# Retention's output and the last feed-forward with 512-wide matmuls throughout, and a feed-forward factor from two fp32r matmuls

## The chip, the cores and the metric

The kernel runs on one core of a Trainium2 chip. Its engines work side by side and are tied together by semaphores: PE (TensorE) multiplies matrices and writes to PSUM, ACT (ScalarE), DVE (VectorE) and POOL (GpSimd) work on elements, and SP issues transfers. PSUM has eight banks here of 128 x 512 float32 values. The metric is the device time of one launch in microseconds, as the median of several runs. Before the change it was 1341.47 us (three runs, 1341.17 to 1342.63).

## The reference

The program is a trunk of four layers on 256 tokens with 1024 features. Each layer does `x += mixer(RMSNorm(x))` and then `x += MLP(RMSNorm(x))`; the mixers are retention (layers 0 and 3), a convolution module (layer 1) and stick-breaking attention (layer 2). The two parts that the change touches are the output projection of retention and the feed-forward:

```python
def retention_mixer(xn, w_in, q_gain, k_gain, gn_w, gn_b, w_out):
    ...
    return (jax.nn.silu(g) * y) @ w_out          # (256, 2048) @ (2048, 1024)

def squared_relu_mlp(xn, w1, w2):                # w1 (1024, 4096), w2 (4096, 1024)
    h = jax.nn.relu(xn @ w1)
    return (h * h) @ w2

def rms_norm(x, w):
    xf = x.astype(jnp.float32)
    y = xf * lax.rsqrt(jnp.mean(xf * xf, axis=-1, keepdims=True) + EPS)
    return (y * w.astype(jnp.float32)).astype(x.dtype)
```

## The kernel before

**Split products.** Every float32 operand of a large product is held as two fp32r parts, a rounded "high" part and the rest, "low". A product is then high x high + high x low + low x high. Weights come in units of 128 x 1024 values (a chunk of two units is one transfer of 1 MB); ACT casts the high part `wh` (L357) and DVE subtracts to get the low part `wl` (L364). Activations are kept transposed, features on the partitions and the 256 tokens along the free axis, as a tile `[high 256 | low 256]`: `z0` to `z7` for the normed input (L446 on ACT, L447 on DVE), `h` for the feed-forward's middle, `y` for the mixer's result (`split`, L382 and L383).

**Two forms of one unit.** A unit of kind "b" has four blocks of 128 input features (`kk`) and two halves of 128 output features (`m`), so eight groups. `mm_b`, the narrow form, does a group as three matmuls with 256 columns each (L511, L512, L513) that all add into one half of one bank. `mm_w`, the wide form, does it as two: `wl` times the high half, 256 columns (L527), and `wh` times both halves at once, 512 columns (L531). The wide form keeps the two halves of the result apart, so a pair of output blocks needs two banks, and `sum_w` adds them afterwards: per bank one ACT copy (L574) and one DVE addition (L575) into an SBUF tile. Both forms stream 768 columns a group.

**Banks.** Two pools of four banks each: `acc` for the large products and `mis` for everything else (transposes, column sums, scores).

**Retention's output** (the end of `retention`, L881 to L889) has four pairs of output blocks, `p` = 0 to 3, and four units each. The units come in the order of `OUT_ORDER`: p 0 and 1 in turn over the four `kb`, then p 2 and 3 in turn. Pairs 0, 1 and 2 are wide in two `acc` banks each, pair 3 is narrow in one. Since `acc` has four banks, pair 2 takes the banks of pair 0. `evac` (in `out_begin`) adds the result to `x` (L899) and makes the next norm's `z` tiles and squares (`norm_pair`); pair 3 makes `z6` and `z7`, which the feed-forward needs for the last quarter of its input features.

**The feed-forward** (`ffn`) makes 16 pairs of 256 middle features from two units each, and then in layers 0 to 2 four pairs of 8 units with `w2` (pairs 0 to 2 wide, pair 3 narrow in layer 0 and three quarters wide, by `pair_x`, in layers 1 and 2). The norm's factor is not applied to the input. In layers 0 to 2 it is multiplied onto the result of `w2`; `norm_rb` makes it, called while pair 2 is traced: POOL adds the two halves of the squares (L485), a float32 matmul with a matrix of -1 sums over the partitions and spreads the sum (L487), and DVE makes the reciprocal. In the last layer it is applied in `act` (L617) to each pair of the middle; it is made by `norm_r` (column sums, L407, after pair 0) and `bcast` (four small matmuls, L414, inside pair 2). Pairs 0 and 1 are computed before it is there: they are narrow, and their results wait ("held") in one `acc` bank each.

**What sets the order.** Within most of this code a planner reorders each engine's instructions when the program is built, by its own costs. `keep_in_program_order` pins an instruction behind the one traced before it on its engine. In `mm_w` the 512-column matmul is always pinned behind the 256-column one of its group; with `keep=True` both are, so the whole stream of a pair is in the written order (from pair 4 of a feed-forward, from pair 2 in the last layer). Parts of the conv and attention mixers have their order written out by hand.

**Constants.** The attention mixer needs four constant 128 x 128 matrices as fp32r (`U`, `m1`, `id`, `neg`). `stick` makes them with four DVE copies (L1355), queued behind an instruction of layer 0's retention (`self.mark`).

Of the kernel before, what the change touches and what calls it, by code (L numbers as in the profile page):

```python
# [9 lines left out]
F32R = mybir.dt.float32r  # L10
# [232 lines left out]
class Trunk:  # L243
    def __init__(self, ctx, tc, xT, w, prm, cst, fin, gn, out):
        self.tc, self.nc = tc, tc.nc
        self.w_d, self.out_d, self.x_d, self.fin_d, self.gn_d = w, out, xT, fin, gn
        pool = lambda name, bufs, **k: ctx.enter_context(tc.tile_pool(name=name, bufs=bufs, **k))
        self.cp = pool("cp", 1)
        self.raw = pool("raw", 3)
        self.wp = pool("wp", 5)  # L250
        self.zp = pool("zp", 1)
        self.big = pool("big", 36)
        self.t2 = pool("t2", 10)
        self.colp = pool("colp", 3)
        self.bc = pool("bc", 2)
        self.prp = pool("prp", 3)
        self.dram = pool("dram", 2, space=bass.MemoryType.DRAM)
        self.acc_p = pool("acc", 4, space=bass.MemoryType.PSUM)
        self.mis_p = pool("mis", 4, space=bass.MemoryType.PSUM)
        self.n = 0  # L260
        self.un = 0
        nc = self.nc
        head = self.cp.tile([P, NP0 + 512], F32, name="head", tag="head")
        self.prm0 = head[:, :NP0]
        self.x = [head[:, NP0:]]
        self.prm = self.cp.tile([P, NPCOL - NP0], F32, name="prm", tag="prm")
        self.cst = self.cp.tile([P, NCCOL], F32, name="cst", tag="cst")
        self.first = [self.raw.tile([P, RAWW], F32, name=f"raw{n}", tag="raw") for n in range(3)]
        self.ones = self.tmp().bitcast(mybir.dt.bfloat16)[:, :512]
        nc.gpsimd.memset(self.ones, 1.0)  # L270
        self.warm(11)

        def weights(n, a, b, queue=nc.sync):
            queue.dma_start(self.first[n][:, a:b], w[n][:, a:b])

        weights(0, 0, 512, nc.scalar)
        nc.sync.dma_start(head[:, : NP0 + S], xT[:, : NP0 + S])
        nc.sync.dma_start(self.x[0][:, S:], xT[:, NP0 + S : NP0 + 512])
        weights(0, 512, 1024)
        for p in range(1, 4):  # L280
            self.x.append(self.cp.tile([P, 512], F32, name=f"x{p}", tag=f"x{p}"))
            nc.sync.dma_start(self.x[p], xT[:, NP0 + p * 512 : NP0 + (p + 1) * 512])
            weights(p // 2, p % 2 * 1024, (p % 2 + 1) * 1024)
        for o in range(UPC):
            weights(2, o * 1024, (o + 1) * 1024)
        n = CCOL["D"]
        nc.sync.dma_start(self.cst[:, :n], cst[:, :n])
        nc.sync.dma_start(self.prm, prm[:, NP0:])
        self.cst_d = cst
        self.id = self.c("id", P)  # L290


# [189 lines left out]
    def norm_rb(self):  # L482
        nc = self.nc
        sq = self.sq[:, :S]
        nc.gpsimd.tensor_add(sq, sq, self.sq[:, S:])  # L485
        ps = self.mis()
        nc.tensor.matmul(ps[:, :S], self.c("m1", P), sq, start=True, stop=True)  # L487
        b = self.bc.tile([P, S], F32, name=self.nm("rb"), tag="rb")
        nc.vector.tensor_scalar(out=b, in0=ps[:, :S], scalar1=-1.0 / D, scalar2=EPS, op0=ALU.mult, op1=ALU.add)
        nc.vector.reciprocal(out=b, in_=b)  # L490
        return b
# [117 lines left out]
    def ffn(self, i, nxt):  # L609
# [22 lines left out]

        held = []
        for p in range(16):
            pw = ("ffn_w1", i, p * 256, self.zs)
            if last and p < 2:
                held.append(self.pair_b(*pw))
            else:
                at = p == 2
                act(self.pair_w(*pw, keep=p >= (2 if last else 4), before=factor if at else None))  # L640
            if last and p == 0:
                with self.tc.high_priority():
                    self.norm_r(False)
# [81 lines left out]
    def retention(self, j, nxt):  # L725
# [69 lines left out]
        for h in range(RH):  # L795
# [31 lines left out]
                )  # L827
            a1 = self.bigt(F32R)
            nc.scalar.copy(a1[:, :P], a[1])
            self.mark = nc.vector.tensor_sub(a1[:, P : 2 * P], a[1], a1[:, :P]).ins  # L830
            A.append((self.split(a[0]), a1))
        y = []
        for h in range(RH):
# [47 lines left out]
        ps = {}  # L881
        for kb, p in OUT_ORDER:
            w = self.unit(("ret_w_out", j, "b", kb, p * 256))
            two = p < 3
            if kb == 0:
                ps[p] = (self.acc(), self.acc()) if two else self.acc()
            (self.mm_w if two else self.mm_b)(ps[p], w, lambda k: y[k], kb * 4, kb == 0, kb == 3)
            if kb == 3:
                evac(p, self.sum_w(ps[p]) if two else ps[p])  # L889


    def out_begin(self, nxt, bias=None):
# [455 lines left out]
    def stick(self, j, nxt):  # L1348
        nc = self.nc
        self.table("natural_log_exp_and_others")  # L1350
        kw = dict(skip_group_check=True)
        Ur, m1r, idr, negr = (self.cp.tile([P, P], F32R, name=f"{k}r", tag=f"{k}r") for k in ("U", "m1", "id", "neg"))
        for t, key in ((Ur, "U"), (m1r, "m1"), (idr, "id"), (negr, "neg")):
            with self.tc.issue_after(self.mark):
                nc.vector.tensor_copy(t, self.c(key, P))  # L1355
        G = {}


# [210 lines left out]
```

## Time and profile before

| | |
|---|---|
| median of 3 runs | 1341.47 us |
| the profiled execution's own time | 1341.68 us |
| its span in the profile | 1339.9 us |
| PE busy | 1329.1 us (99%), 8285 matmuls |
| weight loads of PE busy | 1168.7 us (87%) |
| DVE / ACT / POOL busy | 985.2 / 781.3 / 133.4 us |

The span runs from the first to the last instruction; the own time has 1.78 us around it. PE's row counts a matmul as busy from its issue to its modelled end, so consecutive matmuls overlap in it; a matmul's real price in a stream is the distance from its start to the next start. Rows of the timeline give the start in us, the duration in us, the engine, the line, the operation, the tiles, the shape, and a count where several are merged into one row; a bracket gives idle time before the row and what ended it.

### The profile page before, as it was taken

The numbers are of one execution on the slowest core, as the hardware profiler recorded it, in microseconds if no ns is written. First come the engines' busy times: TensorE is split into PE (matmuls) and PEld (weight loads), VectorE is DVE, ScalarE is ACT, GpSimd is POOL, SyncE is SP. The second block draws the span as 40 slices with busy tenths as digits, with TensorE's granted clock in tenths as the row PEclk, the third lists the DMA queues.
The fourth block names the chain that finished last, engine by engine and source line by source line (L and its number), as shares of the span: only waits on it lengthen the run. The fifth ranks groups of instructions, "written<-read, shape, count | busy, mean of one in ns | idle before, by whom it ended". The sixth has DMA issues, their size and how long they took to land.

```text
span 1339.9 us, 20908 instructions
## 1 busy us (share of the span) xinstructions
PE 1329.1 (99%) x8285; PEld 1168.7 (87%) x8285; DVE 985.2 (74%) x1642; ACT 781.3 (58%) x1205; POOL 133.4 (10%) x123
## 2 busy tenths in 40 slices
PE   9999999999999999999999999999999999999998
PEld 8988888888999898888878898888888888988886
DVE  7977769775688698765787597755697777788543
ACT  7555556764456477744578577744565555555442
POOL 3200002000269110000100010000120000100000
PEclk9999999999999999999999999999999999999999
DMA  7645455555445645555443345555455454555551
GB/s 285 237 178 188 175 183 190 189 190 189 183 164 144 220 167 208 192 191 192 171 178 126 126 169 192 192 191 192 176 182 185 173 188 173 189 189 189 204 188 63
DMA packets 41730, 244.56 MB, mean 183 GB/s; under 512 B 4512, under 2 KB 9248, under 8 KB 14240
## 3 DMA queue, kind: packets, MB, share of 16 engines
q1 hardware_dynamic: 40768, 240.60, 50.2%
q10 hardware_dynamic: 864, 2.62, 0.6%
q8 instruction: 65, 1.06, 0.3%
q14 instruction: 33, 0.27, 0.1%
HBM read 241.27 MB, written 1.93 MB: 182 GB/s over the span
## 4 chain that ended last, share of the span: by engine, by line
PE 98%; DVE 1%; DMA 0%; ACT 0%; SPq 0%; issue 0%; DVEq 0%
PE acc L531 34%; PE acc L527 18%; PE acc L690 7%; PE acc L925 6%; PE acc L927 6%; PE acc L926 6%; PE acc L511 4%; PE acc L513 4%; PE acc L512 4%; PE acc L1227 1%; PE acc L1094 1%; PE mis L816 1%; PE mis L877 1%; DMA raw<-in_w 0%; PE mis L407 0%; PE mis L1466 0%
## 5 line engine op out<-in xcount | busy, mean ns | idle before, releaser
L364 DVE TENSOR_TENSOR wl<-raw,wh 128x1024 fp32r<-128x1024 f32 (+1 forms) x440 | 545.5, 1245 | 239.9 <-ACT wh L357 233.7
L357 ACT CAST wh<-raw 128x1024 fp32r<-128x1024 f32 (+1 forms) x440 | 456.6, 1042 | 352.6 <-PE acc L531 164.9
L531 PE MATMUL acc<-z,wh 128*128 128x512 f32 x1120 | 387.4, 392 | 0.0
L527 PE MATMUL acc<-z,wl 128*128 128x256 f32 x1120 | 310.2, 281 | 0.0
L531 PE MATMUL acc<-big,wh 128*128 128x512 f32 x864 | 298.8, 392 | 0.0
L531 PEld LDWEIGHTS acc<-z,wh 128*128 128x128 f32 x1120 | 208.3, 187 | 44.7
L527 PE MATMUL acc<-big,wl 128*128 128x256 f32 x864 | 238.5, 280 | 0.5 <-DVE t L575 0.5
L527 PEld LDWEIGHTS acc<-z,wl 128*128 128x128 f32 x1120 | 211.0, 189 | 1.7
L531 PEld LDWEIGHTS acc<-big,wh 128*128 128x128 f32 x864 | 161.0, 187 | 34.8
L527 PEld LDWEIGHTS acc<-big,wl 128*128 128x128 f32 x864 | 162.4, 189 | 2.3 <-DVE t L575 1.3
L925 PE MATMUL acc<-wh,z 128*128 128x512 f32 x352 | 138.0, 392 | 0.0
L927 PE MATMUL acc<-wh,z 128*128 128x512 f32 x352 | 137.3, 390 | 0.0
L926 PE MATMUL acc<-wl,z 128*128 128x512 f32 x352 | 137.2, 390 | 0.0
L462 POOL TENSOR_TENSOR t<-t,t 128x512 f32<-128x512 f32 x23 | 36.4, 1582 | 894.8 <-ACT t L457 851.6
L574 ACT COPY t<-acc 128x256 f32<-128x256 f32 x176 | 61.8, 372 | 100.6 <-PE acc L531 99.4
L575 DVE TENSOR_TENSOR t<-acc,t 128x256 f32<-128x256 f32 x176 | 69.1, 421 | 34.8 <-ACT t L574 34.6
L690 PE MATMUL acc<-wh,big 128*128 128x512 f32 x256 | 79.3, 390 | 0.0
L927 PEld LDWEIGHTS acc<-wh,z 128*128 128x128 f32 x352 | 66.1, 188 | 14.8 <-issue 0.8
L925 PEld LDWEIGHTS acc<-wh,z 128*128 128x128 f32 x352 | 66.1, 188 | 13.9 <-issue 0.8
L926 PEld LDWEIGHTS acc<-wl,z 128*128 128x128 f32 x352 | 66.1, 188 | 13.3
L513 PE MATMUL acc<-z,wl 128*128 128x256 f32 x256 | 72.6, 284 | 0.0
L511 PE MATMUL acc<-z,wh 128*128 128x256 f32 x256 | 72.5, 284 | 0.0
(268 smaller groups left out, 1810.7 us busy)
## 6 DMA issues: line engine op xcount, KB each, us to landing
raw<-in_w SPq DMA_DIRECT2D x214, 1024.0 KB, 4.8
big<-in_gn SPq DMA_DIRECT2D x16, 256.0 KB, 5.4
raw<-in_w SPq DMA_DIRECT2D x7, 512.0 KB, 7.8
raw<-hd SPq DMA_DIRECT2D x8, 263.0 KB, 4.7
raw<-hd SPq DMA_DIRECT2D x8, 131.5 KB, 3.1
wh<-in_w ACTq DMA_DIRECT2D x2, 512.0 KB, 6.2
wl<-in_w ACTq DMA_DIRECT2D x2, 512.0 KB, 8.9
hd<-big SPq DMA_DIRECT2D x6, 143.5 KB, 2.2
```

The costliest lines, as they stand in the source:

```text
L357: nc.scalar.copy(hi[:, s], src[:, s])
L364: self.nc.vector.tensor_sub(lo[:, s], src[:, s], hi[:, s])
L511: nc.tensor.matmul(o, wh[:, kk, cs], ah, start=st, stop=False, **kw)
L513: nc.tensor.matmul(o, wl[:, kk, cs], ah, start=False, stop=en, **kw)
L527: mm = nc.tensor.matmul(ps[m][:, :S], wl[:, kk, cs], a[:, :S], start=first and kk == 0, stop=False, **kw)
L531: nc.tensor.matmul(ps[m], wh[:, kk, cs], a, start=False, stop=last and kk == 3, **kw)
L574: nc.scalar.copy(o[:, s], ps[m][:, S:])
L575: nc.vector.tensor_add(o[:, s], ps[m][:, :S], o[:, s])
L690: self.tc.keep_in_program_order(nc.tensor.matmul(ps[t], l, r[:, kk], start=False, stop=kb * 2 + kk == 31 and n == 2, **kw))
L925: nc.tensor.matmul(ps[t], zh[:, s], wh[:, kk], start=k == 0, stop=False, skip_group_check=True)
L926: nc.tensor.matmul(ps[t], zh[:, s], wl[:, kk], start=False, stop=False, skip_group_check=True)
L927: nc.tensor.matmul(ps[t], zl[:, s], wh[:, kk], start=False, stop=k == 7, skip_group_check=True)
```

## The change

- In retention's output all four pairs are wide. Pairs 0 and 1 take two `acc` banks each, pairs 2 and 3 two `mis` banks each.
- In the last feed-forward pairs 0 and 1 are wide too. Their sums by `sum_w` are held in SBUF tiles instead of banks, pair 2's likewise, and the factor is taken inside pair 3 instead of pair 2; the pinned order begins at pair 3.
- `norm_rb` (layers 0 to 2) splits the summed squares into a high and a low fp32r part and sums over the partitions with two fp32r matmuls of 256 columns instead of one float32 matmul.
- The four fp32r constants are made in layer 0's retention after head 0, instead of being traced in `stick`.

```diff
@@ Trunk.__init__
+        self.cr = {k: self.cp.tile([P, P], F32R, name=f"{k}r", tag=f"{k}r") for k in ("U", "m1", "id", "neg")}
@@ norm_rb
         nc.gpsimd.tensor_add(sq, sq, self.sq[:, S:])
+        hl = self.split(sq)
         ps = self.mis()
-        nc.tensor.matmul(ps[:, :S], self.c("m1", P), sq, start=True, stop=True)
+        for e in range(2):
+            nc.tensor.matmul(ps[:, :S], self.cr["m1"], hl[:, e * S : (e + 1) * S], start=e == 0, stop=e == 1)
@@ ffn
         for p in range(16):
-            pw = ("ffn_w1", i, p * 256, self.zs)
-            if last and p < 2:
-                held.append(self.pair_b(*pw))
+            ps = self.pair_w(
+                "ffn_w1", i, p * 256, self.zs, keep=p >= (3 if last else 4),
+                before=factor if p == (3 if last else 2) else None,
+            )
+            if last and not rb:
+                held.append(ps)
             else:
-                at = p == 2
-                act(self.pair_w(*pw, keep=p >= (2 if last else 4), before=factor if at else None))
+                act(ps)
@@ retention, after the scores of a head
-            self.mark = nc.vector.tensor_sub(a1[:, P : 2 * P], a[1], a1[:, :P]).ins
+            nc.vector.tensor_sub(a1[:, P : 2 * P], a[1], a1[:, :P])
+            if j == h == 0:
+                for key in ("U", "m1", "id", "neg"):
+                    nc.vector.tensor_copy(self.cr[key], self.c(key, P))
@@ retention, output
-            two = p < 3
             if kb == 0:
-                ps[p] = (self.acc(), self.acc()) if two else self.acc()
-            (self.mm_w if two else self.mm_b)(ps[p], w, lambda k: y[k], kb * 4, kb == 0, kb == 3)
+                bank = self.acc if p < 2 else self.mis
+                ps[p] = bank(), bank()
+            self.mm_w(ps[p], w, lambda k: y[k], kb * 4, kb == 0, kb == 3)
             if kb == 3:
-                evac(p, self.sum_w(ps[p]) if two else ps[p])
+                evac(p, self.sum_w(ps[p]))
@@ stick
-        Ur, m1r, idr, negr = (self.cp.tile(...) ...)
-        for t, key in ((Ur, "U"), (m1r, "m1"), (idr, "id"), (negr, "neg")):
-            with self.tc.issue_after(self.mark):
-                nc.vector.tensor_copy(t, self.c(key, P))
+        Ur, m1r, idr, negr = (self.cr[k] for k in ("U", "m1", "id", "neg"))
```

More of the change, by code (lines that the diff above doesn't have):

```diff
@@ L1351, in stick @@
         kw = dict(skip_group_check=True)
-        Ur, m1r, idr, negr = (self.cp.tile([P, P], F32R, name=f"{k}r", tag=f"{k}r") for k in ("U", "m1", "id", "neg"))
-        for t, key in ((Ur, "U"), (m1r, "m1"), (idr, "id"), (negr, "neg")):
-            with self.tc.issue_after(self.mark):
-                nc.vector.tensor_copy(t, self.c(key, P))
+        Ur, m1r, idr, negr = (self.cr[k] for k in ("U", "m1", "id", "neg"))
         G = {}
```

## The prediction

> **What bounds the kernel now.** I read the page first, then the chain of work that ended last, then PE's own timeline around the edits.
>
> ```profile
> span 1339.9 us, 20908 instructions
> PE 1329.1 (99%) x8285; PEld 1168.7 (87%) x8285; DVE 985.2 (74%) x1642; ACT 781.3 (58%) x1205; POOL 133.4 (10%) x123
> ...
> PEclk9999999999999999999999999999999999999999
> ...
> PE 98%; DVE 1%; DMA 0%; ACT 0%; SPq 0%; issue 0%; DVEq 0%
> ```
>
> The chain runs through PE for 98% of the span, at the full granted clock. So what counts is PE's own issue: how far apart the matmuls start, and the few places where PE waits. What the other engines gain or lose is free as long as PE is not made to wait. No transfer is added, removed or moved by the change.
>
> **Narrow to wide.** One narrow unit of retention's output, from its first matmul to the start of the next unit, and wide groups of two stretches of another stage, on PE's timeline:
>
> ```profile
> 202.07 0.28 PE L511 MATMUL acc<-big,wh 128*128 128x256 f32 x1
> ...
> 204.82 0.28 PE L513 MATMUL acc<-big,wl 128*128 128x256 f32 x1
> 204.94 0.28 PE L527 MATMUL acc<-z,wl 128*128 128x256 f32 x1
> ...
> 207.07 0.28 PE L527 MATMUL acc<-z,wl 128*128 128x256 f32 x1
> ...
> 978.42 0.63 PE L531 MATMUL acc<-z,wh 128*128 128x512 f32 x2
> ...
> 979.23 0.28 PE L527 MATMUL acc<-z,wl 128*128 128x256 f32 x1
> ...
> 987.21 0.28 PE L527 MATMUL acc<-z,wl 128*128 128x256 f32 x1
> ...
> 990.21 0.63 PE L531 MATMUL acc<-z,wh 128*128 128x512 f32 x2
> 990.68 0.28 PE L527 MATMUL acc<-z,wl 128*128 128x256 f32 x1
> ...
> 1001.28 0.28 PE L527 MATMUL acc<-z,wl 128*128 128x256 f32 x1
> ```
>
> A narrow unit is 24 matmuls from 202.07 to 204.94, 2.87 us, 0.359 a group. From 979.23 to 987.21 lie 23 wide groups: 7.98 / 23 = 0.347 a group, 2.78 a unit. From 990.68 to 1001.28 lie 30: 10.60 / 30 = 0.353 a group, 2.83 a unit. The reader is to see that wide work has two cadences at the same clock, fast (0.347) and slow (0.353), and that one lasts until the order is disturbed: the slow one here starts behind two 512-column matmuls in a row (990.21). Behind the narrow unit it is slow as well: six groups from 204.94 to 207.07, 2.13 / 6 = 0.355. Eight units of retention's output (four a layer) and four of the last feed-forward become wide: 12 x (2.87 - 2.78) = **1.1 us** at the fast cadence, 12 x 0.04 = 0.5 at the slow. I take 1.1, since the narrow runs ahead of these stages are gone too.
>
> [...]
>
> **The bank wait.** Pair 2 of retention's output, in both layers:
>
> ```profile
> 180.87 1.09 PE L531 MATMUL acc<-big,wh 128*128 128x512 f32 x4
> 182.19 0.38 PE L527 MATMUL acc<-big,wl 128*128 128x256 f32 x1 [0.23 <-DVE t L575]
> 182.41 0.40 PE L531 MATMUL acc<-big,wh 128*128 128x512 f32 x1
> ...
> 1130.04 1.09 PE L531 MATMUL acc<-big,wh 128*128 128x512 f32 x4
> 1131.36 0.38 PE L527 MATMUL acc<-big,wl 128*128 128x256 f32 x1 [0.23 <-DVE t L575]
> ```
>
> A fast group is 0.347 and its 256 columns are a third, some 0.12; the 512 columns take 0.23. Four of these from 180.87 end at 181.79, yet the next matmul starts at 182.19: 0.40 lost while `sum_w` of pair 0 empties the banks, and 0.22 to the matmul behind it instead of 0.12. That is 0.5 a layer, **1.0 us** in both. In `mis` pair 2 has nothing to wait for: the last transposes, which used those banks, are over some 8 us earlier.
>
> ```profile
> 172.62 1.04 PE L877 MATMUL mis<-cst,t 128*128 128x128 f32 x8
> ```
>
> Were these banks late after all, the loss would be at most today's 1.0. What is next late is the end of the stage. Pair 3's sum now goes through ACT and DVE before `x` is updated:
>
> ```profile
> 1151.00 0.40 PE L531 MATMUL acc<-big,wh 128*128 128x512 f32 x1
> ...
> 1153.99 0.28 PE L513 MATMUL acc<-big,wl 128*128 128x256 f32 x1
> 1154.11 0.28 PE L511 MATMUL acc<-z,wh 128*128 128x256 f32 x1
> ```
> ```profile
> 1152.30 0.69 DVE L899 TENSOR_TENSOR x<-t,x 128x512 f32<-128x512 f32 x1
> ...
> 1154.44 0.68 DVE L899 TENSOR_TENSOR x<-acc,x 128x512 f32<-128x512 f32 x1
> ...
> 1157.24 1.92 DVE L447 SCALAR_TENSOR_TENSOR z<-x,head,z 128x256 fp32r<-128x256 f32 x2
> ```
>
> The wide pair 2 ends at 1151.40 and its `x` starts at 1152.30, 0.9 later; the narrow pair 3 ends at 1154.27 and its `x` starts 0.17 later. So `z6` and `z7` come 0.73 later against PE. They are ready at 1159.16, 5.05 us after PE begins the feed-forward at 1154.11; then 5.8. Until then PE has the first six of eight input blocks of pairs 0 and 1, 24 groups of 0.347, 8.3 us. That covers it if the planner orders them so; without the cover 0.73 a layer is lost. I take 0.2 in all, between 0 and 1.5.
>
> **The factor of layers 0 to 2.** The float32 matmul stands between two groups:
>
> ```profile
> 215.96 0.39 PE L531 MATMUL acc<-z,wh 128*128 128x512 f32 x1
> 216.18 0.59 PE L487 MATMUL mis<-t,cst 128*128 128x256 f32 x2
> 216.43 0.47 PE L527 MATMUL acc<-z,wl 128*128 128x256 f32 x1
> 216.73 0.40 PE L531 MATMUL acc<-z,wh 128*128 128x512 f32 x1
> ```
>
> From 512 columns to 512 columns it is 0.77 instead of 0.347: it costs 0.42. Two fp32r matmuls of 256 columns cost 0.12 each, 0.24. Three layers gain 3 x 0.18 = **0.5 us**. The split adds one ACT cast and one DVE subtraction, which wait for POOL's sum. What they hold up is the weights' casts and subtractions behind them in both queues:
>
> ```profile
> L383 DVE TENSOR_TENSOR big<-t,big 128x256 fp32r<-128x256 f32 x136 | 52.9, 418 | 0.0
> L382 ACT CAST big<-t 128x256 fp32r<-128x256 f32 x8 | 3.2, 405 | 0.0
> ```
> ```profile
> 488.71 0.81 POOL L485 TENSOR_TENSOR t<-t 128x256 f32<-128x256 f32 x1
> ```
> ```profile
> 492.45 0.67 ACT L574 COPY t<-acc 128x256 f32<-128x256 f32 x2 [2.68 <-PE acc L531]
> ```
> ```profile
> 493.71 0.59 PE L487 MATMUL mis<-t,cst 128*128 128x256 f32 x2
> ```
>
> In layer 1 POOL is done at 489.52, ACT sits idle for 2.68 us then, and PE uses the sum at 493.71: 4.2 us for 0.4 + 0.42 of work. Cost nothing; without that slack PE would wait at most about 1 us a layer.
>
> **The rest.** In the last feed-forward held pairs 0 and 1 add eight ACT and DVE pieces of some 0.4 us to engines busy 58% and 74%; freeing the banks early can only help PE, and the factor is needed one pair later than it is today. The four copies of constants keep their price and move forward:
>
> ```profile
> L1355 DVE CAST Ur<-cst x1: 219/219/219, 107.4 to 107.4; 128x128 fp32r<-128x128 f32 x1
> ```
>
> ```profile
> 76.73 1.23 DVE L364 TENSOR_TENSOR wl<-raw,wh 128x1024 fp32r<-128x1024 f32 x1 [0.97 <-ACT wh L357]
> ```
>
> They are 4 x 0.22 = 0.9 us of DVE some 30 us earlier, where DVE has about that much to spare (0.97 idle before 76.73, behind head 0's scores). Nothing; if none of it were covered, at most 0.9.
>
> **Sum.** 1.1 + 1.0 + 0.5 - 0.2 = 2.4 us off the profiled execution's 1341.68 (span 1339.9 and 1.78 around it): **1339.3**. That execution lies 0.2 above the median of the runs, so about 1339.1 as a median; I say 1339.2.
>
> **The rival on the other side: the feed-forwards fall into the slow cadence.** Today each of them runs fast from the factor on. In layer 1:
>
> ```profile
> L531 PE MATMUL acc<-z,wh x224: 391/391/396, 494.3 to 571.6; 128*128 128x512 f32 x112
> ```
>
> 223 distances in 77.3 us are 0.347. The float32 matmul makes a hiccup (0.30 from 216.43 to 216.73 instead of 0.12), and behind it PE is fast in every layer. Two 256-column matmuls make none; they prolong a run of 256-column matmuls, as a narrow unit does, and behind those it was slow. From the factor on, layer 0 has 14 x 16 + 3 x 64 = 416 wide groups, layers 1 and 2 have 48 more, 464. If the slow cadence sets in there and lasts (the pinned order has nothing that ends it), it costs 0.0066 a group: 2.7, 3.1 and 3.1 us. One such layer gives about 1342, two 1345, all three 1348.2. It decides at once in the two matmuls after L531 and is paid over the whole layer. For it: the run at 204.94, and the doubled 512 columns at 990.21 that suffice. Against it: the same disturbance at 978.42 stands just ahead of the fast stretch, so not each one tips it.
>
> [...] That a run here shows why there are two cadences I can't say.
>
> **Other rivals.** The late `z6` and `z7` stall PE in both layers: 1339.3 + 1.3 = 1340.6. For it speaks that DVE took 1.92 us for the last two `L447`, longer than the 1.4 or so that two additions (0.69 each) take; against it the 8.3 us of cover. Or the change doesn't do what it says: the wide units keep the slow cadence, and it yields 0.5 instead of 1.1: 1339.9. Or stretches that are slow today turn fast, as the 30 groups at 990.68 (0.2 us) and the stages next to the edits; with no loss for `z7` that is 1338.3.
>
> **Chances.** All fast, as summed: 0.42 (its own range 1338.2 to 1340.2). More turns fast: 0.12. Late `z`: 0.06. Slow wide units: 0.04. One slow feed-forward: 0.13; two: 0.10; three: 0.13. A measurement of this kernel can tell about 0.2%, 2.7 us: below 1338.8 is faster, above 1344.2 slower. Faster: the 0.12 and somewhat under half of the 0.42, 0.30. Slower: two or three slow feed-forwards, 0.23, and 0.03 for a stall that I did not see, 0.26. The same: 0.44. The range goes from 1337.6, somewhat under the better case, to 1346.8, which leaves out the three slow feed-forwards and little else.
>
> **What would show it.** Right: no idle time ended by L575 in front of pair 2; no L511 to L513 in retention's output and at the start of the last feed-forward; pairs of L531 0.347 apart through each feed-forward; 0.24 for the two L487. Wrong: L531 x224 in layers 0 to 2 lasting 78.8 instead of 77.3 us (the slow cadence), or idle time of PE ended by L447 near 210 or 1158.

## The result and the profile after

The changed kernel takes 1339.57 us (median of 22 runs, 1338.68 to 1340.44), the kernel before beside it 1341.52 (22 runs, 1340.88 to 1342.63). The ratio is 0.9984, with a 95% interval of 0.9978 to 0.9991. So the change gains about 1.95 us, 0.15%, which is below the 0.2% that the prediction set as its bound for "faster". Forecast were 1339.2 and "the same" as the likeliest case. The profiled execution took 1339.27 us, 2.41 less than the one before, where the sum that was forecast was 2.4. That it fits so closely is luck: the 22 runs spread over 1.8 us, and the medians differ by 1.95. The span fell by 2.72 us, but the time around it grew from 1.78 to 2.12, for a reason that no run shows. The sum was right in its size and only partly in its terms, as the experiments show.

The page of the changed kernel: the span, the busy times, and the chain that ended last by engine.

```profile
span 1337.2 us, 20725 instructions
PE 1327.7 (99%) x8189; PEld 1162.7 (87%) x8189; DVE 984.4 (74%) x1653; ACT 783.6 (59%) x1216; POOL 135.2 (10%) x123
...
PE 98%; DVE 1%; DMA 0%; ACT 0%; issue 0%; DVEq 0%
```

PE is still 98% of the chain. It has 96 matmuls fewer: 12 units of 8 groups each, one matmul less a group. The factor leaves the count as it was, since one float32 matmul shows as two records (three of them are the `x6` of L487 before). What PE waits for, in the view of waits (what waited, for whom, in total, times, longest), behind two waits of 1.3 and 1.0 us that are the same before and after:

```profile
...
PE acc L1102 <- issue: 0.4, 1, 0.4
PE acc L595 <- DVE z L448: 0.2, 1, 0.2
PE mis L415 <- DVE lns L1164: 0.2, 1, 0.2
```

Lines have moved by one to eight: 527 and 531 (the wide matmuls) are now 530 and 534, 575 (the addition of `sum_w`) is 578, 447 (`z`) is 448, 487 (the factor's matmul) is 490. The wait of PE for the addition in front of pair 2 is gone, and the one for `z` at L595 belongs to the conv stage, not to a feed-forward.

PE's timeline at the first matmul of the feed-forward, in layers 0 and 3, and then DVE's in layer 3:

```profile
203.91 0.28 PE L530 MATMUL acc<-z,wl 128*128 128x256 f32 x1
...
1151.74 0.28 PE L530 MATMUL acc<-z,wl 128*128 128x256 f32 x1
```

```profile
1155.60 0.69 DVE L907 TENSOR_TENSOR x<-t,x 128x512 f32<-128x512 f32 x1
...
1157.35 0.87 DVE L448 SCALAR_TENSOR_TENSOR z<-x,head,z 128x256 fp32r<-128x256 f32 x2
```

The feed-forwards begin at 203.91 and 1151.74 instead of 204.94 and 1154.11. `z7` is there at 1158.22, 6.5 us after PE began, where it was 5.05 before; PE does not wait for it.

The factor in layer 0:

```profile
226.18 0.39 PE L534 MATMUL acc<-z,wh 128*128 128x512 f32 x1
226.41 0.28 PE L490 MATMUL mis<-big,m1r 128*128 128x256 f32 x1
226.53 0.28 PE L530 MATMUL acc<-z,wl 128*128 128x256 f32 x1
...
228.39 0.28 PE L490 MATMUL mis<-big,m1r 128*128 128x256 f32 x1
228.50 0.39 PE L534 MATMUL acc<-z,wh 128*128 128x512 f32 x1
```

The two matmuls cost 0.12 and 0.11 us to the next start. The planner put them 2 us apart and 10 us later than the float32 one stood, and PE waits for neither.

Where the time went is read from the start of each stage's first matmul (or of its column sums, or of retention's last transposes) on PE's timeline, in the kernel before and in each other kernel. The table has what each stage added to the difference, in us; the first row holds the start of a launch too, which makes PE up to 0.7 later within the first 10 us in these executions than in the one before. Columns are the changed kernel and experiments that are described below.

| stage | ends in before at | after | e1 | e2 | e3 | e4 | e5 | e10 |
|---|---|---|---|---|---|---|---|---|
| retention 0 to its last transposes | 173.38 | -0.12 | +0.41 | +0.48 | +0.70 | +0.20 | +0.07 | +0.24 |
| retention 0, output | 204.94 | -0.91 | -0.91 | -0.34 | -0.46 | 0 | +0.16 | -0.91 |
| feed-forward 0 | 388.90 | -0.03 | +0.01 | 0 | +2.66 | +0.01 | -0.19 | +0.01 |
| conv | 482.52 | -0.28 | -0.52 | -0.72 | -0.65 | +0.02 | -0.37 | -0.69 |
| feed-forward 1 | 666.21 | -0.13 | 0 | 0 | 0 | -0.01 | -0.13 | 0 |
| attention | 778.86 | -0.06 | -0.07 | 0 | -0.07 | -0.03 | -0.02 | -0.08 |
| feed-forward 2 | 957.12 | -0.20 | 0 | 0 | 0 | 0 | -0.19 | +0.01 |
| retention 3 to its last transposes | 1122.60 | +0.22 | -0.02 | 0 | -0.02 | 0 | +0.41 | -0.02 |
| retention 3, output | 1154.11 | -0.86 | -0.91 | -0.34 | -0.46 | 0 | +0.05 | -0.91 |
| feed-forward 3 | 1339.87 | -0.35 | +1.76 | 0 | +1.70 | -0.21 | +0.06 | -0.40 |
| all | | -2.72 | -0.25 | -0.92 | +3.40 | -0.02 | -0.15 | -2.75 |

Retention's output gives 1.77 of the 2.72 and the last feed-forward 0.35. The factor gives 0.36 in three layers instead of 0.5. The rest, 0.24, comes from places that are not in the sum.

### The profile page after: what moved, and what is told of

The parts are those of the page before. It is cut to its first block, busy times and chain, and to the rows that moved or that the text cites. A ratio compares the mean times of both kernels' runs of the same rounds, so it can differ in the third digit from the quotient of the medians.

```text
span 1337.2 us, 20725 instructions
## 1 busy us (share of the span) xinstructions
PE 1327.7 (99%) x8189; PEld 1162.7 (87%) x8189; DVE 984.4 (74%) x1653; ACT 783.6 (59%) x1216; POOL 135.2 (10%) x123
## 3 DMA queue, kind: packets, MB, share of 16 engines
q8 instruction: 64, 1.05, 0.3%
## 4 chain that ended last, share of the span: by engine, by line
PE 98%; DVE 1%; DMA 0%; ACT 0%; issue 0%; DVEq 0%
PE acc L534 34%; PE acc L530 17%; PE acc L695 7%; PE acc L933 6%; PE acc L935 6%; PE acc L934 6%; PE acc L514 3%; PE acc L516 3%; PE acc L515 3%; PE mis L534 2%; PE mis L530 1%; PE acc L1235 1%; PE acc L1102 1%; PE mis L821 1%; PE mis L885 1%; PE mis L408 0%
## 5 line engine op out<-in xcount | busy, mean ns | idle before, releaser
L534 PE MATMUL acc<-z,wh 128*128 128x512 f32 x1152 | 398.2, 392 | 0.0
L534 PE MATMUL acc<-big,wh 128*128 128x512 f32 x800 | 277.5, 393 | 0.0
L534 PEld LDWEIGHTS acc<-z,wh 128*128 128x128 f32 x1152 | 214.1, 187 | 46.1
L530 PE MATMUL acc<-big,wl 128*128 128x256 f32 x800 | 221.5, 279 | 0.0
L530 PEld LDWEIGHTS acc<-z,wl 128*128 128x128 f32 x1152 | 216.6, 189 | 2.4 <-DVE t L578 0.3
L534 PEld LDWEIGHTS acc<-big,wh 128*128 128x128 f32 x800 | 149.4, 187 | 33.5
L530 PEld LDWEIGHTS acc<-big,wl 128*128 128x128 f32 x800 | 150.3, 189 | 0.7
L578 DVE TENSOR_TENSOR t<-acc,t 128x256 f32<-128x256 f32 x176 | 68.8, 420 | 35.6 <-ACT t L577 35.1
L514 PE MATMUL acc<-z,wh 128*128 128x256 f32 x224 | 63.6, 284 | 0.0
```

The source lines that it names most:

```text
L514: nc.tensor.matmul(o, wh[:, kk, cs], ah, start=st, stop=False, **kw)
L530: mm = nc.tensor.matmul(ps[m][:, :S], wl[:, kk, cs], a[:, :S], start=first and kk == 0, stop=False, **kw)
L534: nc.tensor.matmul(ps[m], wh[:, kk, cs], a, start=False, stop=last and kk == 3, **kw)
L578: nc.vector.tensor_add(o[:, s], ps[m][:, :S], o[:, s])
```

## Experiments: the parts one by one

The theory was that the terms of the sum are the mechanisms: wide groups, the bank wait, the factor. Rivals were the late `z6` and `z7` and the slow cadence of the feed-forwards.

### e1_out: retention's output alone

On the kernel before:

```diff
-            two = p < 3
             if kb == 0:
-                ps[p] = (self.acc(), self.acc()) if two else self.acc()
-            (self.mm_w if two else self.mm_b)(ps[p], w, lambda k: y[k], kb * 4, kb == 0, kb == 3)
+                bank = self.acc if p < 2 else self.mis
+                ps[p] = bank(), bank()
+            self.mm_w(ps[p], w, lambda k: y[k], kb * 4, kb == 0, kb == 3)
             if kb == 3:
-                evac(p, self.sum_w(ps[p]) if two else ps[p])
+                evac(p, self.sum_w(ps[p]))
```

> The kernel before with retention's output alone as in the change (all four pairs wide, pairs 2 and 3 in mis banks). My sum gives it 8 units x 0.09 = 0.7 us for the wide form plus 2 x 0.5 = 1.0 for the bank wait, less 0.2 for the later z6 and z7: 1.5 us faster than before, split evenly between layers 0 and 3. Rival, late z6 and z7 cost their full 0.73 a layer: 0.2 to 0.3 us faster only. Rival, only the wait counts since the wide units keep the slow cadence: 1.1 us.

Measured: 1342.0 us against 1341.63, ratio 1.0007 (0.9998 to 1.0016). The output stages are 0.91 shorter in both layers, yet nothing is left at the end, because the last feed-forward is 1.76 longer. PE's timeline of this kernel, inside pair 2 of that feed-forward:

```profile
1165.67 0.40 PE L531 MATMUL acc<-z,wh 128*128 128x512 f32 x1
1167.53 0.68 PE L414 MATMUL mis<-cst,ry 128*128 128x128 f32 x4 [1.46 <-DVE ry L402]
```

The reader is to see a wait of 1.46 us for the factor, where the kernel before has none. The factor's chain begins with the column sums (L407) on PE, and ends with some ten small steps on DVE, with weight subtractions of 1.2 us between them. First and last of this chain and PE's use of it in the kernel before (PE's and DVE's timeline), and then first and last in this one:

```profile
1161.07 0.95 PE L407 MATMUL mis<-cst,t 128*128 128x1 f32 x8
...
1166.18 0.16 DVE L402 SCALAR_TENSOR_TENSOR ry<-rt,ry 128x2 f32<-128x2 f32 x1
...
1167.93 0.61 PE L414 MATMUL mis<-cst,ry 128*128 128x128 f32 x4
```

```profile
1162.29 0.95 PE L407 MATMUL mis<-cst,t 128*128 128x1 f32 x8
...
1167.23 0.16 DVE L402 SCALAR_TENSOR_TENSOR ry<-rt,ry 128x2 f32<-128x2 f32 x1
```

The chain takes the same 5 us, but it starts 1.2 later, since pair 3's result reaches the squares later (POOL starts them at 1158.25 instead of 1156.86). The factor is ready at 1167.39 instead of 1166.34, 1.05 later, and PE comes for it at 1166.07 (1167.53 less the wait) instead of at 1167.93, 1.86 earlier. The changed kernel meets it one pair later (DVE's and PE's timeline):

```profile
1168.26 0.16 DVE L403 SCALAR_TENSOR_TENSOR ry<-rt,ry 128x2 f32<-128x2 f32 x1
...
1170.70 0.61 PE L415 MATMUL mis<-cst,ry 128*128 128x128 f32 x4
```

There the factor is ready at 1168.42, later still, but PE comes for it 2.28 after that.

### e2_bank and e3_wide: the banks without the wide pair, and the reverse

e2 leaves pair 3 narrow, and takes its bank and pair 2's from `mis`; e3 makes all pairs wide and keeps them in `acc`. Both on the kernel before:

```diff
-                ps[p] = (self.acc(), self.acc()) if two else self.acc()
+                bank = self.acc if p < 2 else self.mis
+                ps[p] = (bank(), bank()) if two else bank()
```

```diff
-            two = p < 3
-                ps[p] = (self.acc(), self.acc()) if two else self.acc()
-            (self.mm_w if two else self.mm_b)(ps[p], w, lambda k: y[k], kb * 4, kb == 0, kb == 3)
+                ps[p] = self.acc(), self.acc()
+            self.mm_w(ps[p], w, lambda k: y[k], kb * 4, kb == 0, kb == 3)
```

> The kernel before with pair 2 of retention's output in two mis banks and pair 3 narrow as before, in one mis bank. This is the bank wait alone. My sum: no idle time ended by the addition of sum_w in front of pair 2, and 1.0 us less in all, 0.5 in each of layers 0 and 3. Rival: PE waits for something else at the same place, or loses it again at the end of the stage, 0 to 0.3 us.

> The kernel before with pair 3 of retention's output wide but all pairs in acc banks, so that pairs 2 and 3 wait for the banks of pairs 0 and 1. This is the wide form alone. My sum: 8 x 0.09 = 0.7 us for the wide units, the wait of 0.5 a layer stays as it is, less 0.2 for z6 and z7: 0.5 us faster. Rival: pair 3 now waits too, for the sum of pair 1 (another 0.2 to 0.5 a layer), and the gain is gone or turns into a loss of 0.3.

Measured: e2 1340.8 us, 0.9994 (0.9985 to 1.0003); e3 1345.44 us, 1.0028 (1.0017 to 1.0039). By the table the banks alone give 0.34 in each output stage and the wide pair alone 0.46; together (e1) 0.91.

In e2 PE no longer waits for the addition of `sum_w`, and what the wait cost is gone whole: 0.49, of which 0.38 lay ahead of the first matmul of pair 2 and 0.11 behind it. But 0.15 comes back as slow groups: without the wait, pair 2's wide units stand in turn with the narrow ones of pair 3, and run slow behind them. One such unit in e2, from its first matmul to the start of the next:

```profile
187.97 0.28 PE L527 MATMUL mis<-big,wl 128*128 128x256 f32 x1
...
190.80 0.28 PE L511 MATMUL mis<-big,wh 128*128 128x256 f32 x1
```

That is 2.83 us, 0.354 a group. In the kernel before, the first 22 groups behind the wait take 7.63 us (182.41 to 190.04), 0.347 each.

e3 was slower for two reasons that lie elsewhere. One is the late factor again (1.70 in the last feed-forward). The other is 2.66 in feed-forward 0, where the groups change their cadence (PE's timeline, and then the rows of one line: count, least, median and largest duration in ns, first and last start):

```profile
222.13 0.39 PE L531 MATMUL acc<-z,wh 128*128 128x512 f32 x1
222.35 0.32 PE L527 MATMUL acc<-z,wl 128*128 128x256 f32 x1
222.52 0.39 PE L531 MATMUL acc<-z,wh 128*128 128x512 f32 x1
...
L531 PE MATMUL acc<-z,wh x207: 395/398/403, 222.9 to 295.7; 128*128 128x512 f32 x104
```

The matmul at 222.35 takes 0.17 to the next start instead of 0.12: some 45 ns of a pause. Before it groups are 0.347 apart; behind it 206 distances in 72.8 us are 0.353. That the pause is the cause isn't shown: e1 and e10 pause longer at the same place of the program, 0.11 us, and stay fast (in e10 the 15 distances from 222.32 to 227.52 are 0.347). The slow cadence goes on through `w2` to the end of the feed-forward and costs what the prediction's rival priced for a layer, 2.7 us, though no run of 256-column matmuls stood before it.

### e4_held: the last feed-forward alone

On the kernel before, the `ffn` part of the diff and nothing else (wide pairs 0 and 1, held in SBUF, the factor inside pair 3):

```diff
-            if last and p < 2:
-                held.append(self.pair_b(*pw))
-            else:
-                at = p == 2
-                act(self.pair_w(*pw, keep=p >= (2 if last else 4), before=factor if at else None))
+            ps = self.pair_w(..., keep=p >= (3 if last else 4), before=factor if p == (3 if last else 2) else None)
+            if last and not rb:
+                held.append(ps)
+            else:
+                act(ps)
```

> The kernel before with the last feed-forward alone as in the change (pairs 0 to 2 wide and held in SBUF, the factor inside pair 3). My sum: 4 units x 0.09 = 0.4 us faster, all of it between the end of layer 3's retention and the column sums and first pairs of the last feed-forward. Rival: the later factor or the extra sums stall PE and it is the same as before.

Measured: 1341.38 us against 1341.39, 1.0001 (0.9992 to 1.001). The stage is 0.21 shorter and the execution started 0.20 later; alone this part can't be told from nothing.

### e5_factor: the factor and the constants alone

The changed kernel with retention's output and the `ffn` part taken back:

```diff
 # retention's output and ffn as before; norm_rb as after:
+        hl = self.split(sq)
-        nc.tensor.matmul(ps[:, :S], self.c("m1", P), sq, start=True, stop=True)
+        for e in range(2):
+            nc.tensor.matmul(ps[:, :S], self.cr["m1"], hl[:, e * S : (e + 1) * S], start=e == 0, stop=e == 1)
```

> The kernel before with the factor of the feed-forwards in layers 0 to 2 alone as in the change (split sum, two fp32r matmuls, constants made early). My sum: 3 x 0.18 = 0.5 us faster, the groups behind it at 0.347. Rival, the cadence: without the float32 matmul's hiccup the feed-forwards run at 0.353 a group, 2.7 to 3.1 us slower for each layer in which it sets in, up to 8.4 us in all.

Measured: 1341.5 us against 1341.63, ratio 1.0 (0.9991 to 1.0009). The three feed-forwards are 0.19, 0.13 and 0.19 shorter, 0.51 in all, what the prediction counted. It is lost again in retention 3 (+0.41), where the factor has no part. The changed kernel loses 0.22 in the same stage. There a stretch of groups that is fast in the kernel before is slow in the changed one; the two, in this order:

```profile
L531 PE MATMUL acc<-big,wh x37: 392/395/395, 1108.7 to 1121.1; 128*128 128x512 f32 x37
```

```profile
L534 PE MATMUL acc<-big,wh x36: 393/398/403, 1106.9 to 1119.3; 128*128 128x512 f32 x36
```

36 distances in 12.4 us against 35 in 12.4. The code there is the same, and in e1, e2, e3, e4 and e10 the stage has no such loss.

### e10_outheld: the change without the factor

Retention's output and the last feed-forward as changed, the factor and the constants as before: the diffs of e1 and e4 together, on the kernel before.

> The change without the factor of layers 0 to 2: retention's output and the last feed-forward together. By stages, from the runs of single parts: 0.91 in each of the two outputs and 0.4 in the last feed-forward, where the factor inside pair 3 takes away the 1.46 us that PE waited for it with the output alone. Sum 2.2 us faster than before, give or take a cadence of 0.2 to 2.7 us in a stage that isn't touched. Rival, the parts do not add: 0.5 or less faster.

Measured: 1339.83 us against 1341.58, 0.9989 (0.998 to 0.9998). That is nearly the whole gain, and by the intervals it can't be told from the changed kernel. So 0.4 (e1's loss), 0.0 (e4) and -0.1 (e5) are what the parts do alone, and -1.75 is what two of them do together. They don't add because the last feed-forward's part does two things. Its four wide units give some 0.2 to 0.4, and its later place for the factor keeps retention's part from being given back at a wait. The last row of the table shows it: +1.76 in e1, -0.21 in e4, -0.40 in e10.

## Experiments: the two cadences

The largest rival was that the feed-forwards fall into the slow cadence. In the changed kernel they did not. The 512-column matmuls of layer 0 behind the factor:

```profile
L534 PE MATMUL acc<-z,wh x187: 390/391/391, 228.5 to 293.0; 128*128 128x512 f32 x187
```

186 distances in 64.5 us are 0.347. The next four kernels ask whether that is luck, and what decides it.

### e6_pinned: the two matmuls pinned side by side at pair 4

```diff
-            nc.tensor.matmul(ps[:, :S], self.cr["m1"], hl[:, e * S : (e + 1) * S], start=e == 0, stop=e == 1)
+            self.tc.keep_in_program_order(
+                nc.tensor.matmul(ps[:, :S], self.cr["m1"], hl[:, e * S : (e + 1) * S], start=e == 0, stop=e == 1)
+            )
...
-                before=factor if p == (3 if last else 2) else None,
+                before=factor if p == (3 if last else 4) else None,
```

> The changed kernel with the two fp32r matmuls of the factor pinned back to back at the start of pair 4, where every matmul around them is pinned too (512, 256, 256, 256, 512 columns in a row, layers 0 to 2). This puts the question of the cadence. If an unbroken run of 256 columns tips PE into the slow cadence and it lasts, 384 to 432 groups a layer x 0.0066 = 2.5 to 2.9 us slower than the changed kernel for each layer, up to 8.2 in all. If not, within 0.3 us of the changed kernel, groups at 0.347.

Measured: 1365.23 us, 1.017 (1.015 to 1.019; ratios are against the kernel before here too, and in all that follow), for a reason of its own. The split was called at pair 4 too, so it was made just there, and PE waited for it. PE's timeline, and then a table by stretch (stretch, length, PE busy and instructions, granted clock, DMA share, GB/s):

```profile
226.52 0.39 PE L536 MATMUL acc<-z,wh 128*128 128x512 f32 x1
231.99 0.58 PE L491 MATMUL mis<-big,m1r 128*128 128x256 f32 x1 [5.08 <-ACT big L383]
232.90 0.58 PE L491 MATMUL mis<-big,m1r 128*128 128x256 f32 x1 [0.33 <-DVE big L384]
233.28 0.41 PE L532 MATMUL acc<-z,wl 128*128 128x256 f32 x1
...
233.91 0.41 PE L532 MATMUL acc<-z,wl 128*128 128x256 f32 x1
```

```profile
226.50:232.00 5.50, 0.42 (x4) 0.97 0.54 195
232.00:238.00 6.00, 5.67 (x18) 0.50 0.00 0
238.00:244.00 6.00, 6.00 (x34) 0.95 0.31 105
```

Behind a wait of 5.08 us the granted clock is 0.50 for the next 6 us, and a group takes 0.63 (233.28 to 233.91) instead of 0.347. So the two waits, 5.4 us together, cost 8.7. The half clock lasted 6.8 us in layer 0 (231.72 to 238.55) and in layer 1, and 3.4 in layer 2; over the whole span the mean is 0.992, against 0.999 in the changed kernel. What sets these lengths the runs don't show.

The feed-forwards are 11.2, 7.2 and 5.5 longer than in the changed kernel. In layer 0, 2.5 of this is the slow cadence, from the half clock to the end:

```profile
L536 PE MATMUL acc<-z,wh x173: 395/398/403, 238.9 to 299.7; 128*128 128x512 f32 x173
```

172 distances in 60.8 us are 0.353. Behind the same two matmuls layers 1 and 2 run at 0.347. Since waits of 0.33 to 0.52 us part the two here and the half clock lies behind them, this doesn't tell what an unbroken run does, and e9 asks again. The run does show what the slack in the prediction's factor step is worth: 1 us a layer was its bound without cover, and here the waits and the half clock cost 5.5 to 8.7, because the whole order of PE was pinned behind the split.

### e7_narrow5: a run of 256-column matmuls inside each feed-forward

In the changed kernel pair 5 of layers 0 to 2 is narrow, with every matmul pinned in the written order:

```diff
-            ps = self.pair_w(...)
+            if p == 5 and not last:
+                ps = self.pair_n("ffn_w1", i, p * 256, self.zs)
+            else:
+                ps = self.pair_w(...)
```

> The changed kernel with pair 5 of the feed-forward in layers 0 to 2 narrow and pinned: 48 matmuls of 256 columns in a row ahead of a pinned wide stream. By itself the narrow form costs 3 x 2 x 0.09 = 0.6 us. If the slow cadence follows a narrow run, as it did at 204.94 in the trace of before, and lasts to the end of the feed-forward, it adds 0.0066 x 352 to 400 groups = 2.3 to 2.6 us a layer, 7.6 in all: 8.2 us slower than the changed kernel. If the slow cadence ends by itself, 0.6 to 1.5 us slower.

Measured: 1346.63 us, 1.0039 (1.0026 to 1.0051), which is 7.06 over the changed kernel's 1339.57. The three layers are 2.55, 2.88 and 2.89 longer than in the changed kernel. Behind the narrow pair, in layer 0:

```profile
L534 PE MATMUL acc<-z,wh x159: 395/398/404, 238.0 to 293.8; 128*128 128x512 f32 x159
```

158 distances in 55.8 us, 0.353, to the end. The narrow pair itself costs 16 x 0.012 = 0.2 of it. In layer 1 it is 157 distances in 55.4 (517.4 to 572.8), 0.353 too. In all three layers this run of 48 matmuls with 256 columns makes everything behind it slow, to the end of the feed-forward.

### e8_reset: the same with a float32 matmul behind each narrow pair

```diff
         return ps   # end of pair_n, before it:
+        self.tc.keep_in_program_order(
+            nc.tensor.matmul(self.mis()[:, :S], self.c("m1", P), self.c("cos", S), start=True, stop=True)
+        )
```

> The kernel with pair 5 narrow in layers 0 to 2 (which ran 7 us slower than the changed kernel), and one float32 matmul of 256 columns, its result unused, pinned behind each narrow pair. It asks whether the slow cadence is a state that a pause of PE ends. If it is: groups at 0.347 from there, the narrow pairs cost 0.6 and the three float32 matmuls 3 x 0.42 = 1.3, so about 1341.5, some 5 us less than without them. If the slow cadence has another cause (the order of units, other engines, banks), the float32 matmuls only add: about 1348.

Measured: 1340.59 us, 0.999 (0.9981 to 0.9998). The kernel does three matmuls more than e7 and is 6.0 us faster. Behind the float32 matmul, in layer 0:

```profile
238.31 0.59 PE L561 MATMUL mis<-cst 128*128 128x256 f32 x2
238.55 0.47 PE L530 MATMUL acc<-z,wl 128*128 128x256 f32 x1
238.86 0.40 PE L534 MATMUL acc<-z,wh 128*128 128x512 f32 x1
...
L534 PE MATMUL acc<-z,wh x160: 391/391/396, 238.9 to 294.0; 128*128 128x512 f32 x160
```

159 distances in 55.1 us, 0.347 again. Each layer is 0.63 longer than in the changed kernel: 0.2 for the narrow pair and 0.42 for the float32 matmul, its price in the prediction. So here the hiccup of a float32 matmul (0.31 from 238.55 to 238.86) puts PE back to the fast cadence, and the kernel before has one at the head of each of these feed-forwards. The change takes it out.

### e9_pinned6: the two matmuls side by side, with the split made in time

The split is made at pair 2, and the two fp32r matmuls stand pinned together at pair 6:

```diff
+    def norm_rb_split(self):   # the POOL addition and the split, called at p == 2
+    def norm_rb(self, hl):     # the two matmuls, pinned, and the rest, called at p == 6
-                before=factor if p == (3 if last else 2) else None,
+                before=factor if p in ((3,) if last else (2, 6)) else None,
```

> The changed kernel with the factor's split where the change has it, and its two fp32r matmuls pinned back to back at the start of pair 6, when the split is long done (in the run with them at pair 4 PE waited 3 to 5 us for it). Layers 0 to 2. If an unbroken run of 256 columns (512, 256, 256, 256, 512) tips PE: 320 to 368 groups x 0.0066 = 2.1 to 2.4 us a layer, up to 7 us over the changed kernel. If it takes more than that to tip it, within 0.5 us of the changed kernel.

Measured: 1342.43 us, 1.0006 (0.9997 to 1.0014). Layers 0 and 2 are as in the changed kernel, and layer 1 is 2.84 longer. Layer 0 and then layer 1, the two matmuls and the groups around them:

```profile
238.07 0.40 PE L494 MATMUL mis<-big,m1r 128*128 128x256 f32 x2
...
L539 PE MATMUL acc<-z,wh x159: 391/391/396, 237.8 to 292.9; 128*128 128x512 f32 x159
...
502.11 0.62 PE L539 MATMUL acc<-z,wh 128*128 128x512 f32 x2
...
514.93 0.40 PE L494 MATMUL mis<-big,m1r 128*128 128x256 f32 x2
...
L539 PE MATMUL acc<-z,wh x194: 387/398/403, 502.3 to 570.8; 128*128 128x512 f32 x194
```

In layer 0 PE is fast before the two and fast behind them. In layer 1 it is slow from 502.3 on, 12.6 us before they come, right behind two 512-column matmuls in a row (502.11), as at 990.21 in the kernel before, and stays slow behind them (193 distances in 68.5 us, 0.355 with the 0.24 of the two in it, 0.354 without). So two 256-column matmuls side by side neither start the slow cadence nor end it.

In the changed kernel layer 1 was near the same edge:

```profile
L534 PE MATMUL acc<-z,wh x187: 392/395/400, 505.6 to 570.1; 128*128 128x512 f32 x187
```

The same two 512-column matmuls stand there at 501.97, the groups behind them are slow, and from 505.6 on they are fast: 186 distances in 64.5 us are 0.347. The factor's two matmuls stood alone at 503.49 and 505.50. In e5, which has two as well, the layer turns fast too (204 distances from 499.7 to 570.8 are 71.1 us, 0.349 with all of this in it); in e9, which has none there, the slow stretch goes on to the end (200 in 70.9, 0.354). So in the changed kernel it ends behind the second one and in e9 not at all, and why the first one doesn't end it isn't known. The changed kernel's layer 1 is fast by the place of one matmul that the planner chose. That is luck, as far as the prediction goes.

## Experiments: going further

### i1_ffn0x: layer 0's last pair of `w2` three quarters wide

```diff
-            if p < 3 or i == 0:
+            if p < 3:
-                ps = self.pair_w(*pw, keep=True) if p < 3 else self.pair_b(*pw)
+                ps = self.pair_w(*pw, keep=True)
```

> The changed kernel with the last pair of layer 0's second matrix three quarters wide, as layers 1 and 2 have it, instead of narrow. 6 units x 0.09 = 0.5 us faster than the changed kernel if the end of the layer is reached no later; the two narrow units that remain end it as before. Rival: the extra sum in front of the last addition delays x and the conv module's first z tiles, and the gain is lost there: 0.

Measured: 1342.02 us, 1.0005 (0.9997 to 1.0014). The profiled execution took 1340.60, 1.4 less than the median, and shows 1.29 of the 2.45 that the median lies over the changed kernel; what the slower executions lose beside it isn't shown. Up to the last units of `w2` the wide form gains 0.64. Then PE loses 1.84 where the conv stage starts, and the layer is 1.20 longer:

```profile
386.52 0.28 PE L516 MATMUL acc<-z,wl 128*128 128x256 f32 x1
387.49 0.38 PE L514 MATMUL acc<-z,wh 128*128 128x256 f32 x1 [0.69 <-ACT z L447]
```

This is the late `z` that the run's rival expected, at a place where PE has no other work: 0.97 from one start to the next instead of 0.12. The other 1.0 goes to the next matmul and to the column sums behind it, which come late as well. What retention's output could afford, with the last pair's sum hidden behind six input blocks of the feed-forward, this stage can't.

### i2_qkwide: layer 0's first six pairs wide

```diff
-                ... (self.pair_w if j else self.pair_b)("ret_w_in", ...)
+                ... self.pair_w("ret_w_in", ...)
```

> The changed kernel with the six narrow query and key pairs of layer 0's retention wide as well (12 units). 12 x 0.09 = 1.1 us faster than the changed kernel, all of it before the sums over heads at 59.8 us. Rival: at the start the engines that cast and subtract are the bound or the banks are, the twelve extra sums come on top, and it is the same or up to 1 us slower.

Measured: 1348.74 us, 1.0049 (1.0037 to 1.0062). PE waits 6.86 us for banks near the start, where wide pairs need twice as many. Its timeline, and the table by stretch:

```profile
37.57 0.55 PE L530 MATMUL acc<-z,wl 128*128 128x256 f32 x1 [6.86 <-DVE t L578]
```

```profile
30.70:37.50 6.80, 0.00 (x1) 0.55 0.76 300
37.60:42.00 4.40, 4.40 (x15) 0.54 0.21 82
```

Here too the granted clock is about half behind the wait, 0.54 for 4.4 us. ACT had copied these banks by 31.5, but the additions that empty them (L578) came only at 37.0, behind weight subtractions and other work in DVE's queue. So both halves of the rival hold, the banks and the engine that subtracts, and the kernel lost 9 us instead of up to 1. In retention's output the wide form paid 0.46 a stage even in occupied banks (e3), and 0.91 with free ones.

## Why the prediction was right, point by point

**The wide units.** Counted: 0.09 a unit. The last feed-forward's four gave 0.35 in the whole change and 0.40 in e10 (0.36 counted), 0.21 alone. Retention's four a layer gave 0.46 alone (e3; 0.36 counted). With these falls the rival by which wide units stay slow.

**The bank wait.** Counted: 0.5 a layer. The wait itself cost 0.49, and that is what e2 removed; its stage shows 0.34, because 0.15 went to wide units that ran slow behind narrow ones. That is why banks and wide pair together give 0.91, where the two alone add to 0.80: with pair 3 wide there are no narrow units left between. The wait had also been a pause behind which groups were fast (0.347 for the 22 of them before), which the prediction didn't see. For the whole stage 0.86 was counted and 0.91 and 0.86 came.

**The late `z6` and `z7`.** Counted: 0.2 lost in all. PE did not wait for them, since 24 groups lie ahead, so nothing was lost at that place. But pair 3's result is later against PE than the 0.73 that was counted: `z7` 1.4 (6.5 us after PE's start instead of 5.05), and `x` itself 3.5 (1155.60 against 1151.74 is 3.86 after PE's start, 1154.44 against 1154.11 was 0.33), because a weight subtraction of 1.75 us stands ahead of pair 3's sum on DVE (1153.16) and one of 1.22 between `x` and `z7`. What is late next is the factor of the last layer. The weak step is "the factor is needed one pair later than it is today", told as a help and costed at nothing: the mechanism was named, but not that the output's gain hangs on it. Without it PE waits 1.46 us (e1), and the two times 0.9 of the output stages are given back. An edit that looked like a detail decides whether the largest term of the sum is kept.

**The factor.** Counted: 0.18 a layer, 0.5 in all. Alone it gave 0.19, 0.13 and 0.19 (e5). In the whole change layer 0 gave only 0.03. There the weight load of a later pair waited for a sum to empty its bank (PE's weight loads, changed kernel):

```profile
215.20 0.19 PEld L530 LDWEIGHTS acc<-z,wl 128*128 128x128 f32 x1 [0.32 <-DVE t L578]
```

With it two matmuls are 0.40 apart instead of 0.23 and the next two 0.22 instead of 0.12, 0.27 in all; e10, without the factor, has a smaller loss at a weight load, 0.11, at another place (221.16), for which the view names no releaser. The difference is the 0.16 that is missing. This wait is no row of PE itself, which is why the view of PE's waits doesn't list it.

**The rest.** Outside the sum stand 0.28 gained in conv (PE's wait for `lns` fell from 0.4 to 0.2, and not all of it is found), 0.06 in attention, 0.12 at the start, and 0.22 lost in retention 3 to a slow stretch. Each kernel of the table whose layer 0 differs from before gained 0.3 to 0.7 in conv, whatever the edit was, and e4, whose layer 0 is the same, did not; that the conv stage gets another order from the planner each time would fit, and isn't shown. The moved constants showed no cost. The planner put their copies at 17.9 to 18.9 us, some 90 us earlier than before and not the 30 that the prediction expected. Behind that, PE gains 0.2 against the kernel before, in two steps of 0.1 near 24 and 36 us, in the changed kernel and in e5, and keeps its distance from there to the end of the stage; e1 to e4 and e10 have no such steps. Why is open.

**The rival on the other side.** The slow cadence exists and has the price that was given: 2.7 us in layer 0 (e3), 2.55 to 2.89 a layer with the narrow pair's 0.2 (e7). Its point of decision was wrong: "in the two matmuls after L531". They don't tip it (e9). A run of 256-column matmuls does (e7, in all three layers). In e3 it sets in behind a pause of 45 ns, and in layer 1 of e9 behind two 512-column matmuls in a row, which the prediction had named as enough at 990.21 and not at 978.42. The prediction was right that the change takes away what guarded the feed-forwards. The changed kernel came out fast without the guard, in layer 1 by luck: there the slow cadence had set in.

## What to carry to other kernels

When a stage gets shorter, look one step beyond the tile that comes late: list the chains that start in the old stage and end in the next one (here `z`, column sums, factor), and ask at which matmul PE meets each of them. Parts of a change that each measure as nothing alone can be worth nearly 2 us together, so a part is judged with its partner (e1 and e4 against e10). In a stream of short matmuls a cheaper instruction may take away a pause that was useful (three of 0.42 us saved 6.0 here, e8 against e7); compare the distances from start to start over a whole stage, and not only at the edit.

## What the runs showed of the hardware

- PE's stream of 256- and 512-column matmuls with a weight load each ran in two cadences at the same granted clock of 1.00 (kernel before, 979.23 to 987.21 and 990.68 to 1001.28), 0.347 and 0.353 us a group, and kept the one it was in for 77.3 us (fast, kernel before, layer 1) and 72.8 us (slow, e3). A run of 48 matmuls of 256 columns started the slow one in three layers of three (e7); behind a pause of 45 ns it set in and cost 2.66 us (e3), while longer pauses, 0.11 us, left the fast one (e1, e10). The pause of one float32 matmul, 0.42 us, ended it and saved 6.0 us in three layers (e8 against e7). Why there are two stays open.
- Waits of PE of 5.4 us, 5.08 of them in one piece, cost 3.3 more behind them, with the granted clock at 0.50 for 6.8 us (e6); after 6.86 us it was 0.54 for 4.4 us (i2).
- A wait for a PSUM bank showed on PE's weight load alone: 0.32 us there, 0.27 lost, and no row in the view of PE's waits (changed kernel, 215.20).
